# Probabilities transposed in 32x32 blocks by VectorE, value products over 32 rows, and a new order of the mixing stage

## The chip, the cores and the metric

The kernel runs on one core of a Trainium2 chip. It is one launch, and the metric is the device time in microseconds of that launch. The core's engines work side by side, each through its own queue in order: TensorE multiplies matrices into PSUM (eight banks of 128 x 512 float32), VectorE and ScalarE read PSUM and SBUF, GpSimd works on SBUF, and SyncE (SP) and GpSimd issue DMA transfers. They wait for each other by semaphores.

## The reference

One layer of an encoder with 512 tokens of width 1024: a half-weighted SwiGLU FFN, a mixing stage, a second such FFN, and a final RMSNorm. The mixing stage projects the normalized tokens once, gives 512 columns to a Fourier mixer and the rest to attention with eight query heads and two key/value heads of 64, and projects both back. Cut to the mixing stage and what attention computes:

```python
x = x + 0.5 * swiglu(rms_norm(x, ffn1_norm), ffn1_w_gate, ffn1_w_up, ffn1_w_down)
u = rms_norm(x, mix_norm) @ w_in
f_out = fourier_mixer(u[..., :512], fnet_w, fnet_b)
a_out = gqa_attention(u[..., 512:1024], u[..., 1024:1152], u[..., 1152:], q_norm, k_norm)
x = x + concatenate([f_out, a_out]) @ w_out
x = x + 0.5 * swiglu(rms_norm(x, ffn2_norm), ffn2_w_gate, ffn2_w_up, ffn2_w_down)
...
# gqa_attention, for a block of 128 queries (q and k normalized per head and rotated):
scores = einsum('bqhgd,bkhd->bhgqk', q_blk, k) * 64 ** -0.5
p = softmax(scores, axis=-1)
out = einsum('bhgqk,bkhd->bqhgd', p, v)
```

## The kernel before

All products are made with float32r operands that are split into a high part and a low rest (`.h` and `.l` operations; the helper `lows`, line 123, is the subtraction), so that a product is three matmuls: high x high, high x low, low x high (`product`, lines 164 to 166). The two FFNs hold x transposed, 128 features by 512 tokens in a tile; their larger groups use a seven-product scheme of 256 columns (line 429). They are the first 335 and the last 339 us of the program.

The mixing stage is written as some 640 small named operations, and the string `ORDER` names all of them in the order in which they are emitted; on each engine, DMA queues too, the instructions stand in that order. An operation's name tells what it does: `k.0` to `k.7`, `q0.0` and so on are the eight steps of a projection (three matmuls each), `q0.pq` sums of squares for a head's norm (four matmuls of two columns, in two passes each), `f00.0` and `f00.1` the halves of a Fourier projection (12 matmuls of 256 columns each, lines 1063 to 1065), `d..`, `map.` and `c..` the transform over positions and channels, `y0.0` to `y7.7` the steps of the output projection; `wq0.r`, `.h`, `.l` load a weight chunk and split it.

Attention goes by pairs: `t` (0 to 3) numbers query heads within a key/value head, `b` (0 or 1) is the key/value head, and `c` is one of four blocks of 128 queries. So there are 32 score tiles of 128 queries by 512 keys.

- `s{t}{b}{c}`: two matmuls of 512 columns (lines 1188, 1189) give a score tile in a PSUM bank.
- `m`: VectorE takes the negated maximum of the tile (line 1194) and multiplies it by the row's factor in `sc` (line 1195).
- `e`: ScalarE makes the exponentials (line 1202) into SBUF and sums them into `z`.
- `t{t}{b}{kc}`: TensorE transposes, for one block of 128 keys, the four query blocks of a head (four transposes of 128 x 128, line 1214) into a bank.
- `h`, `l`: ScalarE casts the bank into the high part `ph` (line 1219), VectorE subtracts for the rest `pl` (line 123).
- `v{t}{b}{kc}`: two matmuls of 512 columns (line 1257) with the stationary tile `vst`, which holds the values of one key block, high in columns 0 to 63 and low in 64 to 127; four key blocks accumulate in one bank.
- `o.c`, `o.a`, `z.r`, `z.w`, `z.p`, `r.m`, `r.h`, `r.l`: add the two halves, divide by the sums (GpSimd spreads them in `z.w`, TensorE transposes them), and split the result for the output projection.

The values are projected transposed, scaled by a row `n1.rb` that `n1.t` and `n1.b` make with four transposes and a copy, and transposed (`vt`, `vp`). GpSimd has little to do in the stage: powers (`.s1`, line 949), four copies, three transfers. PSUM banks come from one pool of eight and are handed out by `bank_for` and given back by `read`.

Of the kernel before, what the change touches and what calls it, by code (L numbers as in the profile page):

```python
# [37 lines left out]
HI_DVE = ("f0", "f1")  # L38
# [5 lines left out]
wk.r wq0.r wv.r cos wk.h wk.l wq0.h k.0 k.1 k.2 k.3 k.4 wv.h k.5 wq0.l k.6 wq1.r k.7 k.sq q0.0 wq1.h n1.c  # L44
k.rc n1.m k.sw n1.p q0.1 q0.2 q0.3 q0.4 wq1.l q0.5 wq2.r n1.t q0.6 q0.7 wq2.h q1.0 k.rs k.pq wv.l q0.sw
n1.b v.0 v.1 k.s0 k.s1 wq2.l q0.rc f2.r wq3.r q0.rs q0.ah q0.bh k.s2 v.2 kw v.3 v.4 v.5 v.6 q0.sq q0.al
q0.bl v.7 vt kp wq3.h km q1.1 wq3.l q0.pq f0.r q0.s0 k1.0 k0.0 k0.1 q1.2 q1.3 q1.4 q1.5 k1.2 k0.2 vp q1.6
q1.7 k0.3 s003 s001 s000 k1.1 k1.3 s010 f1.r v0.h v0.l q0.s1 q0.s2 f0.h m001 m003 s002 q1.sw m002 m010 q1.sq
q1.sd q1.pq e002 m000 v1.h e000 e001 e003 q2.0 q2.1 q2.2 q1.s0 q1.s1 f0.l q1.rc q1.rs v1.l q2.3 q2.4 q1.bh
q2.5 q2.6 q2.7 q2.sw t001 e010 f1.h f1.l q2.rc t000 q3.0 s012 h000 l000 s011 m011 t002 h002 h001 m012 q1.ah  # L50
q1.al q2.sq q3.1 q3.2 q3.3 q3.4 q3.5 q3.6 q1.bl q3.7 s013 l002 e011 v000 e012 f2.h l001 v001 q2.sd q3.sw
q2.rs t003 m013 q2.ah q3.rc q3.sq v002 e013 q2.bh f2.l s100 q1.s2 m100 s102 h003 q3.sd e100 f00.0 t010 f3.r
q2.bl h010 q2.pq l003 q2.s0 q2.s1 t013 m102 e102 s101 m101 f00.1 f00.u q2.al v003 l010 e101 t011 h011 q3.rs
s103 t012 f02.0 h013 l011 z0.r o00.c o00.a q3.bh v010 v011 m103 h012 l012 q3.pq q3.s0 l013 e103 s110 m110
s201 q3.ah s111 q3.bl v012 v013 o01.c t100 m111 h100 l100 e111 o0.r t101 h101 t102 h102 o01.a fw.r f02.1
e110 s112 m112 e112 z0.w pos q2.s2 l102 f01.0 s113 l101 z0.p m113 e113 s203 r0.m f02.e s200 m200 v100 v101
t103 t110 f01.1 r0.h h103 l103 z1.r f02.h v102 f01.u e200 q3.al q3.s1 v103 o10.c t112 m201 h110 r0.l h112
s202 m202 l110 t113 m203 f03.0 f03.1 v110 f3.h q3.s2 o10.a e201 s210 f03.e f3.l t111 l112 f10.0 f02.l h113
h111 l111 e202 f10.1 f03.h e203 s211 v111 m210 o2.r fw.h e210 t200 h200 t202 l113 m211 v112 s300 l200 v113
h202 t201 f10.u h201 l202 o11.c s212 m212 e212 s213 z1.w e211 f12.0 fw.l l201 f12.1 m300 e300 m213 e213  # L60
o11.a z1.p r1.m s301 v200 t203 r1.h f03.l h203 f12.e l203 f12.h z2.r z2.w v201 v202 t211 s302 m302 t210 h210
l210 s303 m303 h211 l211 v203 o20.c o20.a t212 h212 m301 f11.0 f13.0 e302 s311 l212 f12.l o0.h o0.l r1.l
t213 f11.1 f11.u m311 v210 v211 f13.1 h213 l213 f13.e e303 v212 s310 d00 m310 e301 t302 o1.r o1.h o1.l t301
f13.h f13.l e310 v213 o21.c t300 o21.a h302 l302 map0 map0.h map0.l d10 h300 l300 map1 z2.p d00.h map1.h
d00.l e311 t303 r2.m map1.l h303 l303 v300 s312 h301 m312 d20 d01 o2.h s313 d11 l301 v301 v302 v303 m313
e312 d01.h d01.l c0.s o2.l e313 t312 d11.h d11.l o30.c d31 o30.a h312 l312 o4.r c0.c c0.q c0.o t311 d10.h
t310 h311 h310 l310 d10.l d20.h d21 d20.l l311 c0.h c0.l d30 t313 c1.c d21.h d21.l o3.r c1.s c1.q d30.h v310
c1.o d31.h d31.l v311 v312 y1.0 h313 l313 c2.s z3.r z3.w c1.h o6.r d30.l c2.q c2.c y0.0 c2.o c2.h y2.0 c3.s
c3.q v313 r2.h c1.l z3.p c2.l c3.c c3.o y1.1 y2.1 y2.2 y0.1 r2.l y0.2 c3.h c3.l y2.3 y0.3 y1.2 y0.4 y0.5
y0.6 o31.c o31.a r3.m r3.h y1.3 y1.4 r3.l y0.7 o3.h y1.5 y2.4 y0.x y2.5 y2.6 o3.l y1.6 o5.r y1.7 o4.h y0.q  # L70
o4.l y1.x y1.q y2.7 o5.h o5.l y3.0 y1.a y3.1 y3.2 y3.3 y3.4 y3.5 y3.6 y3.7 y1.h o6.h o6.l y3.x y3.q y4.0
y4.1 y4.2 y2.x y2.q y4.3 y5.0 y4.4 y4.5 y4.6 y3.h y3.l o7.r y5.1 y5.2 y5.3 y4.7 y4.x y4.h y2.a y3.a o7.h
y6.0 o7.l y0.h y5.4 y5.5 y4.l y5.6 y4.q y4.a y5.7 y6.1 y6.2 y0.l y6.3 y6.4 y5.x y7.0 y6.5 y2.h y6.6 y6.7
y6.x y1.l y2.l y7.1 y6.q y7.2 y7.3 y7.4 y7.5 y7.6 y5.q y7.7 y6.h y6.l y5.h y5.l y5.a y7.x y7.q y6.a y7.h
y7.a y7.l
# [8 lines left out]
def encoder(ctx, tc, A, out):  # L84
# [15 lines left out]
    pp = ctx.enter_context(tc.tile_pool(name="psum", bufs=8, space=bass.MemoryType.PSUM))  # L100

    def bank(name):
        return pp.tile([P, S], F32, tag="bank", name=name)
# [18 lines left out]
    def lows(lo, src, hi):  # L122
        nc.vector.tensor_tensor(out=lo, in0=src, in1=asf(hi), op=ALU.subtract)  # L123
# [44 lines left out]
    class Norm:  # L168


        def __init__(self, n):
            self.n = n
            self.acc = tp.tile([P, S], F32, tag="acc", name=f"acc{n}")
            self.r = cp.tile([P, 4], F32, name=f"r{n}")
            self.ms = cp.tile([P, 4], F32, name=f"ms{n}")
            self.rb = cp.tile([P, S], F32, tag="rb", bufs=2, name=f"rb{n}")
# [628 lines left out]
    with tc.tile_pool(name="mix", bufs=1) as mp, tc.tile_pool(name="mixt", bufs=1) as mt:  # L805
# [36 lines left out]
        def read(name):  # L842
            held[name][1] -= 1
            if not held[name][1]:
                spare.append(held.pop(name)[0])
# [765 lines left out]
```

## Time and profile before

| | |
|---|---|
| time, median of 3 runs | 837.93 us (837.79 to 838.09) |
| the profiled execution's own time | 837.96 us |
| its span, first to last instruction | 836.2 us |
| mean granted TensorE clock | 0.999 |
| HBM read / written | 111.83 MB / 2.10 MB |
| mixing stage, within the span | 335.6 to 497.4 us |

The page gives busy time by engine; PE is TensorE's matmuls, PEld its weight loads, DVE VectorE, ACT ScalarE, POOL GpSimd. A group of instructions has its line, engine, operation, out<-in, shapes and count, then busy us and mean ns of one, then idle time before it and what ended that. On TensorE and VectorE, instructions overlap their successors, so the distance from start to start is shorter than the duration. The chain of waits goes back from the last instruction to what released each; a row there has a start, the time on the chain, and the line.

### The profile page before, as it was taken

Reading aid. Unit: us, or ns where it says so; the run is one execution under the profiler, and the core shown is the slowest. Engines: PE = TensorE matmul, PEld = TensorE weight load, DVE = VectorE, ACT = ScalarE, POOL = GpSimd, SP = SyncE. Lnnn points to the kernel's source line nnn. Section 1 sums busy time; section 2 is a strip of 40 time slices with the busy share of each in tenths; the row PEclk is TensorE's granted clock in tenths of the full one; section 3 lists DMA queues with packets and bytes.
Section 4 is the critical chain, followed back from the end, with each engine's and each line's share of the span. In section 5 each row is a group of like instructions: output and inputs, shape, how many; then the busy total and the mean of one; then the engine's idle time right before and its main releaser. Section 6 shows DMA issues by size and latency. Waiting matters only on the chain.

```text
span 836.2 us, 13649 instructions
## 1 busy us (share of the span) xinstructions
PE 829.4 (99%) x5418; PEld 752.3 (90%) x5418; DVE 603.4 (72%) x923; ACT 461.9 (55%) x770; POOL 62.5 (7%) x69
## 2 busy tenths in 40 slices
PE   9999999999999999999999999999999999999997
PEld 7888998899989998889999888899988999899986
DVE  7977884578656867699999478878755885578563
ACT  7654763366434644677776446546533663356452
POOL 0111000000000000222000000110000000000001
PEclk9999999999999999999999999999999999999999
DMA  7787765468365423414020326777554674456122
GB/s 253 189 199 191 199 187 147 117 159 226 97 169 151 121 58 114 151 51 146 26 76 26 100 57 170 187 182 197 165 154 125 179 206 131 116 167 189 45 78 101
DMA packets 46110, 117.16 MB, mean 140 GB/s; under 512 B 5216, under 2 KB 9952, under 8 KB 45920
## 3 DMA queue, kind: packets, MB, share of 16 engines
q1 hardware_dynamic: 38128, 92.57, 33.5%
q0 software_dynamic: 7648, 23.47, 16.4%
q8 instruction: 42, 0.69, 0.3%
q10 hardware_dynamic: 272, 0.26, 0.1%
q14 instruction: 20, 0.16, 0.1%
HBM read 111.83 MB, written 2.10 MB: 136 GB/s over the span
## 4 chain that ended last, share of the span: by engine, by line
PE 99%; issue 0%; DVE 0%; POOLq 0%; POOL 0%; ACT 0%
PE r L429 23%; PE q L429 11%; PE dn L166 9%; PE dn L164 9%; PE dn L165 9%; PE p L429 6%; PE mix L164 4%; PE mix L166 3%; PE mix L165 3%; PE gu L766 3%; PE gu L164 3%; PE gu L165 3%; PE gu L166 3%; PE mix L1257 2%; PE mix L1214 2%; PE mix L1188 1%
## 5 line engine op out<-in xcount | busy, mean ns | idle before, releaser
L429 PE MATMUL r<-rt,ring 128*128 128x256 f32 x1686 | 204.9, 276 | 0.0
L429 PEld LDWEIGHTS r<-rt,ring 128*128 128x128 f32 x1686 | 198.5, 188 | 0.9
L165 PE MATMUL dn<-at,ring 128*128 128x512 f32 x295 | 114.8, 389 | 0.0
L166 PE MATMUL dn<-at,ring 128*128 128x512 f32 x295 | 114.8, 389 | 0.0
L164 PE MATMUL dn<-at,ring 128*128 128x512 f32 x295 | 114.8, 389 | 0.0
L429 PE MATMUL q<-rt,ring 128*128 128x256 f32 x840 | 106.6, 276 | 0.0
L374 ACT CAST ring<-s 128x1024 fp32r<-128x1024 f32 x70 | 73.5, 1050 | 58.3 <-DVE s L394 51.5
L581 DVE SCALAR_TENSOR_TENSOR gx<-dn,gx 128x512 f32<-128x512 f32 x61 | 42.1, 691 | 81.1 <-PE dn L166 81.1
L429 PEld LDWEIGHTS q<-rt,ring 128*128 128x128 f32 x840 | 100.4, 188 | 0.0
L123 DVE TENSOR_TENSOR ring<-s,ring 128x1024 fp32r<-128x1024 f32 x70 | 85.3, 1219 | 0.6 <-ACT ring L374 0.6
L156 ACT CAST ring<-raw_dn 128x768 fp32r<-128x768 f32 (+2 forms) x48 | 40.7, 852 | 75.6 <-PE dn L165 70.5
L166 PEld LDWEIGHTS dn<-at,ring 128*128 128x128 f32 x295 | 55.4, 188 | 11.5
L165 PEld LDWEIGHTS dn<-at,ring 128*128 128x128 f32 x295 | 55.4, 188 | 11.1
L164 PEld LDWEIGHTS dn<-at,ring 128*128 128x128 f32 x295 | 55.4, 188 | 11.0
L346 POOL DMA_DIRECT2D s<-in_wgu x35 | 30.1, 861 | 423.5 <-DVE ring L123 146.7
L429 PE MATMUL p<-rt,ring 128*128 128x256 f32 x420 | 53.3, 276 | 0.0
L123 DVE TENSOR_TENSOR ring<-raw_dn,ring 128x768 fp32r<-128x768 f32 (+2 forms) x48 | 46.7, 977 | 7.1 <-ACT ring L156 7.1
L429 PEld LDWEIGHTS p<-rt,ring 128*128 128x128 f32 x420 | 50.2, 188 | 0.0
L123 DVE TENSOR_TENSOR ring<-raw_g,ring 128x1024 fp32r<-128x1024 f32 x35 | 42.6, 1217 | 0.0
L123 DVE TENSOR_TENSOR at<-u,at 128x512 fp32r<-128x512 f32 x35 | 24.2, 693 | 20.3 <-ACT at L484 20.2
L472 DVE TENSOR_TENSOR u<-g,u 128x512 f32<-128x512 f32 x35 | 24.0, 687 | 19.8 <-ACT u L469 19.8
L374 ACT CAST ring<-raw_g 128x1024 fp32r<-128x1024 f32 x35 | 36.8, 1051 | 0.0
(312 smaller groups left out, 1523.0 us busy)
## 6 DMA issues: line engine op xcount, KB each, us to landing
s<-in_wgu SPq DMA_DIRECT2D x70, 256.0 KB, 4.2
s<-in_wgu POOLq DMA_DIRECT2D x35, 512.0 KB, 5.7
raw_g<-in_wgu SPq DMA_DIRECT2D x35, 512.0 KB, 4.0
raw_dn<-in_wd SPq DMA_DIRECT2D x44, 384.0 KB, 3.9
raw_u<-in_wgu SPq DMA_DIRECT2D x35, 256.0 KB, 4.1
raw_gu<-in_wgu SPq DMA_DIRECT2D x12, 512.0 KB, 3.5
raw_o<-in_wo SPq DMA_DIRECT2D x8, 512.0 KB, 3.6
raw_dn<-in_wd SPq DMA_DIRECT2D x5, 448.0 KB, 4.2
```

The source lines that it names most:

```text
L123: nc.vector.tensor_tensor(out=lo, in0=src, in1=asf(hi), op=ALU.subtract)
L156: nc.scalar.copy(hi[:, :n, :], raw[:, :n, :])
L164: nc.tensor.matmul(ps, whi, mhi, start=first, stop=False)
L165: nc.tensor.matmul(ps, whi, mlo, start=False, stop=False)
L166: nc.tensor.matmul(ps, wlo, mhi, start=False, stop=last)
L346: nc.gpsimd.dma_start(out=blocks(t), in_=up, accum_op=ALU.add)
L374: nc.scalar.copy(ts[0], src)
L429: nc.tensor.matmul(ps[:, c], a[:, ks], b[:, i, c], start=first and i == 0 and o == 0, stop=i == KH - 1 and o == 2, skip_group_check=not fi ...
L472: nc.vector.tensor_tensor(out=self["u"], in0=self["g"], in1=self["u"], op=ALU.mult)
L581: nc.vector.scalar_tensor_tensor(out=x[d][:, t], in0=ps[:, t], scalar=0.5, in1=x[d][:, t], op0=ALU.mult, op1=ALU.add)
L766: nc.tensor.matmul(pss[c], w[:, k % 2, c], m[k], start=k == 0 and m is hh and w is hi, stop=k == KD - 1 and w is lo,)
L1214: nc.tensor.transpose(pts[n][:, c * P : (c + 1) * P], prob[t, b, c][:, kc * P : (kc + 1) * P], ident)
```

## The change

What it does, all in the mixing stage but for the banks:

- Transposes of probabilities leave TensorE. `x{t}{b}{c}` is one VectorE instruction that transposes each 32x32 block of an exponentials tile, from SBUF to SBUF. `h` and `l` now read that tile, and write into `its`, which holds the eight tiles of a set: key/value head `b`, two query heads, four query blocks.
- `p{st}`, one for each of four sets, takes the place of 64 value products: 128 matmuls, each over 32 rows (32 keys), with a stationary tile of 32 x 128 and 256 moving columns (8 tiles x 32 queries), on rows 0 to 31, 32 to 63, 64 to 95 and 96 to 127 in turn. Row group `a` has queries 32a to 32a+31 of each block, and accumulates in its own bank `quad[:, a]`. The instruction's tile is 32 x 128, and its position in the array the row group's.
- The stationary values must lie in each of the four row groups: `vr{v}.{a}` copies `stage[v]` into `vrep` with four transfers on GpSimd's queue, 16 for each value head. `vrep` and `its` exist once.
- `m` is one instruction: it multiplies the score tile by the (negated) factor, in its bank, and keeps the minimum. `e` then has the constant scale -1.
- Values are scaled after their transpose (`vm`, by column `n1.r`); `n1.t` and `n1.b` are gone.
- `LOWS_POOL` gives 23 of the 32 probability differences, eight weight differences of 1024 columns and one of 512 to GpSimd; `z.w` goes to ScalarE; `HI_DVE` names other casts for VectorE.
- The eight banks are fixed tiles, four of them one tile `quad`; all stages rotate over them.
- cos, sin, and buffers of the early part share room with the tables of the late part, and `ORDER` is another.

```diff
-HI_DVE = ("f0", "f1")
+LOWS_POOL = """
+001 010 012 013 100 103 110 111 112 113 200 201 202 203 211 212 300 301 302 303 310 311 312 f1 f2 fw o0 o1 o2 wq2
+wq3 wv
+""".split()
+SUMS_ACT = """
+z0 z1 z2 z3
+""".split()
+HI_DVE = """
+300 302 o3 o5 wq2 wv
+""".split()
...
-    pp = ctx.enter_context(tc.tile_pool(name="psum", bufs=8, space=bass.MemoryType.PSUM))
+    pp = ctx.enter_context(tc.tile_pool(name="psum", bufs=1, space=bass.MemoryType.PSUM))
+    quad = pp.tile([P, 4, S], F32, name="quad")
+    quads = [quad[:, i] for i in range(4)]
+    singles = [pp.tile([P, S], F32, name=f"bank{i}") for i in range(4)]
+    turn = singles[1:] + quads + singles[:1]
...
+            def spread(a):
+                for i in range(4):
+                    src, dst = slice(32 * i, 32 * i + 32), slice(32 * a, 32 * a + 32)
+                    nc.gpsimd.dma_start(
+                        out=vrep[dst].rearrange("p (c i) e -> p c i e", i=4)[:, :, i],
+                        in_=stage[v][src].rearrange("p c o e -> p c (o e)"),
+                    )
...
-                nc.vector.tensor_reduce(out=mx, in_=sps[n], axis=AX.X, op=ALU.max, negate=True)
-                nc.vector.tensor_tensor(out=mx, in0=mx, in1=f, op=ALU.mult)
+                nc.vector.tensor_scalar(
+                    out=sps[n], in0=sps[n], scalar1=f, scalar2=None, op0=ALU.mult, op1=ALU.min, accum_out=mx
+                )
...
-                for c in range(4):
-                    nc.tensor.transpose(pts[n][:, c * P : (c + 1) * P], prob[t, b, c][:, kc * P : (kc + 1) * P], ident)
...
+                nc.vector.transpose(turned[n], probs[n])
+
+            op(f"h{n}")(lambda: (nc.vector.tensor_copy if n in HI_DVE else nc.scalar.copy)(ph, turned[n]))
+            op(f"l{n}")(lambda: lows(pl, turned[n], ph, nc.gpsimd if n in LOWS_POOL else nc.vector))
...
+            @op(f"p{st}")
+            def _():
+                all_quads(f"p{st}", 4)
+                for j in range(16):
+                    for o in range(2):
+                        for a in range(4):
+                            rows = slice(32 * a, 32 * a + 32)
+                            nc.tensor.matmul(
+                                quad[:, a, : 8 * 32], vrep[rows, j], its[rows, o, :, 32 * j : 32 * j + 32],
+                                start=j == 0 and o == 0, stop=j == 15 and o == 1, skip_group_check=True,
+                            )
...
-                w = vst[:, b, kc].rearrange("p a e -> p (a e)")
-                for i, p in enumerate(parts[n]):
-                    nc.tensor.matmul(outs[t, b], w, p, start=kc == 0 and i == 0, stop=kc == 3 and i == 1)
```

How the new order moves instructions shows best in three places. The first is TensorE's queue in the middle of attention. Before (`mix` are PSUM banks, `ks` the keys, `qa` and `qb` the queries, `ph` and `pl` the transposed probabilities' parts, `e` the exponentials):

```order
L1188 MATMUL mix_3411<-ks_3420,qb_3714 128x512
L1189 MATMUL mix_3411<-ks_3421,qb_3714 128x512
L1257 MATMUL mix_3416<-ph_3964,vst 128x512
L1257 MATMUL mix_3416<-pl_3966,vst 128x512
L1257 MATMUL mix_3416<-ph_3947,vst 128x512
L1257 MATMUL mix_3416<-pl_3975,vst 128x512
L1214 MATMUL mix_3409<-ident,e_3853 128x128
L1214 MATMUL mix_3409<-ident,e_3919 128x128
L1214 MATMUL mix_3409<-ident,e_3893 128x128
```

And in the change, at the second set of value products (`bank` and `quad` are banks; line 1239 is the score product, 1278 the value products, 1319 the transpose of the sums):

```order
L1239 MATMUL bank_72<-ks_3315,qb_3329 128x512
L1240 MATMUL bank_72<-ks_3316,qb_3329 128x512
L1278 MATMUL quad<-its,vrep 128x256 x128
L1239 MATMUL bank_70<-ks_3315,qb_3329 128x512
L1240 MATMUL bank_70<-ks_3316,qb_3329 128x512
L1319 MATMUL bank_71<-ident,zw_4127 128x128 x4
L1239 MATMUL bank_73<-ks_3315,qb_3331 128x512
```

Value products stood in pairs, one pair for each transposed tile; now 128 of them stand together, and the first can start only when all eight tiles of the set are split.

The second place is VectorE's queue in the same part, before:

```order
L1194 TENSOR_REDUCE mx_3981<-mix_3413 128x1
L1195 TENSOR_TENSOR mx_3981<-mx_3981,sc 128x1
L123 TENSOR_TENSOR qb_3955<-rot_q_3827,qb_3955 64x512
L1194 TENSOR_REDUCE mx_4000<-mix_3411 128x1
L1195 TENSOR_TENSOR mx_4000<-mx_4000,sc 128x1
L123 TENSOR_TENSOR pl_4005<-mix_3409,ph_4003 128x512
```

and in the change, ahead of the third set (`x` is the block-wise transposed tile, `fo` a channel sum of the Fourier mixer, `el` its rest, `ring` the buffer of its positions):

```order
L1245 TENSOR_SCALAR bank_72,mx_4614<-bank_72,sc 128x512
L1263 STREAM_TRANSPOSE x_4616<-e_4584 128x512
L1245 TENSOR_SCALAR bank_71,mx_4620<-bank_71,sc 128x512
L1263 STREAM_TRANSPOSE x_4758<-e_4596 128x512
L1245 TENSOR_SCALAR bank_73,mx_4760<-bank_73,sc 128x512
L1307 RECIPROCAL zall<-zall 128x8
L1263 STREAM_TRANSPOSE x_4782<-e_4618 128x512
L136 TENSOR_TENSOR el_3326<-fo_4607,eh_3322 128x512
```

A maximum with its small product and a difference per tile became a minimum and a transpose per tile; most differences are gone from this queue.

The third place is GpSimd's queue, where they went. In the change, between the first and the third set (`more` and `raw_o` belong to an output weight):

```order
L136 TENSOR_TENSOR its<-x_4199,its 128x512
L136 TENSOR_TENSOR its<-x_4224,its 128x512
L136 TENSOR_TENSOR more<-raw_o_3922,more 128x1024
L1071 DMA vrep<-vst 32x4x128 x4
L136 TENSOR_TENSOR its<-x_4384,its 128x512
L1071 DMA vrep<-vst 32x4x128 x4
L136 TENSOR_TENSOR its<-x_4406,its 128x512
```

Before, GpSimd's queue between the tables' transfers and the second FFN held one power and three copies of sums. Now differences stand among the transfers that replicate the second value head, and the transfers wait until the second set's products have read the first.

More of the change, by code (lines that the diff above doesn't have):

```diff
@@ L54 @@
[L54 to L58, printed above, removed]
@@ L833, in op @@
             return put
[L836 removed]
+        spare, held = [(b, any(b is q for q in quads)) for b in turn], {}
         def bank_for(name, readers=1):
[L839 to L840 removed]
+            i = next((i for i, b in enumerate(spare) if not b[1]), 0)
+            held[name] = [spare.pop(i), readers]
+            return held[name][0][0]
         def read(name):
```

284 lines of the change are left out of this document (147 added, 137 removed).

## The prediction

> **What bounds the kernel now.** I read the page's busy times and chain first, then a table of three stretches of the mixing stage, then TensorE's waits.
>
> ```profile
> PE 829.4 (99%) x5418; PEld 752.3 (90%) x5418; DVE 603.4 (72%) x923; ACT 461.9 (55%) x770; POOL 62.5 (7%) x69
> ...
> PE 99%; issue 0%; DVE 0%; POOLq 0%; POOL 0%; ACT 0%
> ```
> ```profile
> 335.60:381.40 45.80, 45.80 (x233) 38.45 (x232) 38.08 (x70) 33.00 (x56) 9.12 (x4) 1.00 0.28 94
> 381.40:455.10 73.70, 73.70 (x527) 67.70 (x527) 69.36 (x148) 56.73 (x119) 7.82 (x9) 1.00 0.24 77
> 455.10:497.40 42.30, 42.30 (x192) 35.13 (x191) 24.41 (x34) 17.02 (x26) 0.00 (x0) 1.00 0.25 75
> ```
> ```profile
> PE busy L705 <- DVE halves L735: 1.0, 1, 1.0
> ```
>
> The columns of the second fence are the stretch, its length, and busy time of TensorE, its weight loads, VectorE, ScalarE and GpSimd. The mixing stage runs from 335.6 to 497.4, 161.8 us, and TensorE is busy in all of it; its only wait for another engine in the whole program is 1.0 us at the start. So a microsecond of TensorE work that goes is a microsecond gained, as long as the others keep up. Stretch A (the projections) and C (the output projection) have slack: VectorE is busy 38.08 of 45.80 and 24.41 of 42.30. Stretch B, from the first Fourier projection to the last value product, has little: VectorE is busy 69.36 of 73.70, 94%. B cannot become much shorter unless VectorE gets rid of work there. I cost the FFN stages and the fixed banks at nothing: TensorE's instructions there are the same in the same order over the same eight banks, and it waits for nobody. VectorE and ScalarE swap a few operations in the first FFN; if a reused bank came late for that, a matmul would wait for one more eviction, 0.6 us (VectorE's step, below), a few times at most.
>
> **TensorE's prices.** From the chain of waits (start, time on the chain, line) and the groups:
>
> ```profile
> 379.55 0.44 PE mix L1214 x4
> 379.99 0.47 PE mix L1257 x2
> 380.46 0.24 PE mix L1188
> ...
> 383.21 0.79 PE mix L935 x8
> ...
> 405.99 0.11 PE mix L1064
> ```
> ```profile
> L1214 PE MATMUL mix<-ident,e 128*128 128x128 f32 x128 | 18.1, 273 | 0.0
> L1257 PE MATMUL mix<-ph,vst 128*128 128x512 f32 x32 | 13.0, 406 | 0.0
> L1257 PE MATMUL mix<-pl,vst 128*128 128x512 f32 x32 | 12.6, 392 | 0.0
> ...
> L429 PE MATMUL q<-rt,ring 128*128 128x256 f32 x840 | 106.6, 276 | 0.0
> ```
>
> A transpose takes 0.109 us of the chain (0.44 for four), a matmul of 512 columns 0.23, one of 256 columns 0.113 (the rows alternate between 0.11 and 0.12). The group's mean ns are longer, because matmuls overlap; the chain has the time that each takes from the next. Removed: 128 transposes of probabilities, 14.0 us; 64 value products, 14.7; four transposes of n1's row, 0.44. Added: 512 matmuls over 32 rows and 256 columns. Nothing in this trace has 32 rows; every group says 128*128. Bounds from the nearest row, the 256-column matmul: if four of them, on disjoint quarters of the array and in four banks, run side by side, 512 x 0.113 / 4 = 14.5 us; if they run one behind the other, 512 x 0.113 = 57.9 us. I take 14.5: it equals the 14.7 of the value products that they replace, which is the same number of multiplications on a full array, and row groups, banks and replicated values are separate for all four. The other end is a rival. The switch between 32 and 128 rows, eight times, is not in the trace either; bounds are nothing and the overlap that would be lost once, 0.276 - 0.113 = 0.16 us, so up to 1.3 us, of which only the pair in C, 0.3 us, lies where TensorE sets the end.
>
> [...]
>
> With these prices TensorE's work in A is 48 projection steps of three matmuls (33.1), five small sums of 0.79 (4.0), two transposed tiles (0.9) and eight score tiles of two matmuls (3.7): 41.6 us. In B: 192 Fourier matmuls (21.7), 24 score tiles (11.0), positions, maps and channels (10.5), one small sum, three transposed tiles (2.1), 13 output steps (9.0), three of the four sets of value products (10.9): 65.2. In C: the fourth set (3.6), 51 output steps (35.2), 0.4: 39.3. The sum is 146.1, where the same count for the kernel before gives 160.9 against 161.8 in the trace.
>
> **VectorE.** Its instructions overlap too, so the price is the distance between starts:
>
> ```profile
> 440.56 0.68 DVE L123 TENSOR_TENSOR pl<-mix,ph 128x512 fp32r<-128x512 f32 x1
> 441.16 0.68 DVE L1194 TENSOR_REDUCE mx<-mix 128x1 f32<-128x512 f32 x1
> 441.87 0.16 DVE L1195 TENSOR_TENSOR mx<-mx,sc 128x1 f32<-128x1 f32 x1
> 441.95 0.68 DVE L123 TENSOR_TENSOR pl<-mix,ph 128x512 fp32r<-128x512 f32 x1
> ...
> 443.75 1.22 DVE L123 TENSOR_TENSOR ring<-raw_o,ring 128x1024 fp32r<-128x1024 f32 x1
> 444.88 0.42 DVE L123 TENSOR_TENSOR ring<-mix,ring 128x255 fp32r<-128x255 f32 x1
> ```
> ```profile
> L1194 DVE TENSOR_REDUCE mx<-mix 128x1 f32<-128x512 f32 x32 | 21.8, 682 | 1.2 <-PE mix L1189 1.1
> ...
> L987 DVE COPY kw<-sc 128x512 f32<-128x512 f32 x1 | 0.4, 427 | 0.0
> ```
>
> A difference (hi/lo split) of 512 columns costs 0.60, of 1024 columns 1.13, a maximum with its small product 0.79. The new ones are not in the trace. A 32x32 block transpose of 512 columns lies between a copy (0.43) and a maximum with its exposed end (0.71); I take 0.60, as the differences have. The scaled minimum, one instruction over the same bank in place of two, lies between 0.60 and 0.79; I take 0.70. In B, by the order of the change, that makes 28 transposes more (+16.8), 20 probability differences fewer because GpSimd has them (-12.0), three weight differences of 1024 and one of 512 fewer (-4.0), 24 minima for 23 maxima (-1.4), and +3.0 for pieces that moved between stretches (three more channel splits, one more channel sum, two casts, less small ones): +2.4, so 69.4 becomes 71.8. **VectorE has more to do in B than TensorE, 71.8 against 65.2.** B now lasts at least 71.8; if VectorE idles for the same 4.3 us as now, 76.1. I take the middle, 74.0. What is late then is each set of value products: it waits for the splits of all eight tiles of a set, and scores and output steps stand behind it in TensorE's queue. ScalarE (56.73 of 73.70) keeps its count of operations, and SP its transfers.
>
> **GpSimd** takes the differences over, and issues the copies that replicate the values. Its rows:
>
> ```profile
> 367.45 2.54 POOL L949 TENSOR_TENSOR sc<-sc,mhalf 128x8 f32<-128x8 f32 x1 [6.33 <-DVE sc L945]
> 384.88 1.64 POOL L949 TENSOR_TENSOR sc<-sc,mhalf 128x8 f32<-128x8 f32 x1 [14.88 <-DVE sc L945]
> ...
> 390.02 0.61 POOL L1239 COPY zw<-z 128x512 f32<-128x512 f32 x1 [3.51 <-ACT qb L973]
> ...
> 391.19 0.55 POOL L1369 DMA_DIRECT2D pos<-in_pos  x1
> ...
> 403.07 1.03 POOL L1239 COPY zw<-z 128x512 f32<-128x512 f32 x1 [9.04 <-DVE z L1234]
> ```
> ```profile
> L1390 POOL TENSOR_TENSOR gx<-gx,rb 128x256 f32<-128x256 f32 x2 | 1.5, 744 | 2.4 <-ACT rb L246 2.4
> ```
> ```profile
> s<-in_wgu SPq DMA_DIRECT2D x70, 256.0 KB, 4.2
> ```
>
> The copies are 32 issues of some 0.55 us (the pos row), 18 us of GpSimd's time. The first sixteen are early. The other sixteen overwrite the first value head's copies, so they wait for the second set's products, and the third set waits for them: 16 x 0.55 = 8.8 us and a landing of about 4, beside 13 us of TensorE's work from one set to the next, so they hide, barely.
>
> A two-input operation of 256 columns took 0.744, so 512 columns lie between that and 1.49; I take 1.34, and 2.5 for 1024. In B that is 22 probability tiles, the half-size weight and four weights, 41 us of 74: it fits, but the rows show something else. The same power takes 1.64 or 2.54, the same copy 0.61 or 1.03: GpSimd is held by something while VectorE is busy. If VectorE is held in turn, some 26 of its operations in B read two SBUF tiles; each would meet a busy GpSimd 41 times in 74 and wait half of its 1.34: 9.6 us. The other bound is nothing. VectorE's maxima do not spread (682 mean) because GpSimd is idle now. I take a third, 3.2. B becomes 77.2.
>
> The sum: A 45.8 to 41.6 (-4.2), B 73.7 to 77.2 (+3.5), C 42.3 to 39.3 (-3.0), a switch in C (+0.3): -3.4. From the profiled execution's 837.96 us (span 836.2; the median of the runs is 837.93) that gives **834.6**: 15 us less work for TensorE, of which VectorE and GpSimd take back three quarters.
>
> **Rivals.**
> *GpSimd and VectorE hold each other* in B, and the kernel is slower. With the full 9.6 us and all the idle time, B lasts 85.7, +12.0: 837.96 - 4.2 + 12.0 - 3.0 + 0.3 = 843.1. It decides from B at 80.6. For it speak the spread of GpSimd's rows and the 94%; against it, that only 26 of VectorE's operations read SBUF twice. [...]
>
> *The 32-row matmuls do not run side by side.* Each has a weight load of its own (5418 loads for 5418 matmuls), and the matmul of two columns shows the least that such a pair takes: 0.79 / 8 = 0.099. With that price the sets cost 512 x 0.099 = 50.4, 35.9 more than assumed: B 65.2 + 26.9 = 92.1, C 48.3, A 41.6, 182.0 in place of 161.8: 858. With 0.113 each, 866. Against it stands only the layout of the operands.
>
> *VectorE runs ahead*: block transposes nearer 0.43, no lock, and work done in A's slack. Then TensorE's sum holds, 146.1 scaled by 161.8 / 160.9 to 146.9: 823.1. For it: 7.7 us of VectorE's idle time in A. Against: that slack is early, before scores exist.
>
> **How the numbers follow.** The forecast 0.50, held by each other 0.22, not side by side 0.13, running ahead 0.15. A measurement tells 0.2%, 1.7 us, from no change. The forecast's own range, from B at 71.8 plus nothing to B near 84, is 829 to 841: 0.40 faster, 0.08 same, 0.02 slower. The first rival gives 0.04 same and 0.18 slower, the second 0.13 slower, the third 0.15 faster. Faster 0.55, same 0.12, slower 0.33. The range for 8 in 10 leaves out the second rival and a little at both ends: 824 to 846.
>
> **What would show it.** Starts of the new matmuls 0.03 us apart, 3.6 us a set, against 0.1 apart. TensorE with idle time in B, before the sets of value products, ended by VectorE or GpSimd, 8 to 15 us of it; VectorE busy for all of B; none in A and C. Block transposes near 0.60 from start to start; GpSimd's differences near 1.34, and VectorE's two-SBUF differences longer than 0.68 where GpSimd is at work. I am wrong if TensorE has no idle time, if the sets take over 5 us each, or if the FFN stages move by over 1 us.

## The result, and the profile after

The changed kernel takes **969.73 us** (967.42 to 971.27, four runs) against 837.86 (837.72 to 838.09): ratio 1.157, 95% interval 1.1545 to 1.1598. The forecast was 834.6, with 846 as the upper end.

The page after, busy time by engine and the chain's share by engine:

```profile
PE 872.2 (90%) x5734; PEld 765.8 (79%) x5734; DVE 614.6 (63%) x927; ACT 457.9 (47%) x770; POOL 127.1 (13%) x129
...
PE 77%; DVE 12%; ACT 4%; issue 3%; DMA 3%; SPq 0%; POOL 0%; DVEq 0%; POOLq 0%; ACTq 0%
```

TensorE was 99% of the chain before. Now 23% of it is other engines or waiting for them. Where that lies shows in a table of the three stages (length; busy time of TensorE, weight loads, VectorE, ScalarE, GpSimd, each with its number of instructions; granted clock, DMA share, GB/s). Before:

```profile
0.00:335.60 335.60, 334.61 (x2188) 303.29 (x2189) 239.36 (x344) 181.00 (x291) 22.29 (x29) 1.00 0.58 160
335.60:497.40 161.80, 161.80 (x948) 141.27 (x947) 131.85 (x250) 106.74 (x200) 16.94 (x13) 1.00 0.25 81
497.40:836.20 338.80, 332.99 (x2285) 307.73 (x2283) 232.20 (x329) 174.18 (x281) 23.26 (x27) 1.00 0.55 148
```

After:

```profile
0.00:386.15 386.15, 352.17 (x2189) 308.29 (x2189) 240.09 (x344) 180.97 (x291) 22.17 (x29) 1.00 0.51 139
386.15:574.20 188.05, 166.81 (x1263) 141.90 (x1262) 139.31 (x252) 101.28 (x197) 81.55 (x73) 0.92 0.29 80
574.20:969.50 395.30, 353.24 (x2285) 315.60 (x2283) 235.24 (x332) 175.69 (x283) 23.35 (x27) 0.98 0.47 127
```

The two FFN stages, which the change does not touch but for their banks, have the same numbers of matmuls (2188 and 2189 in the records of the first, 2285 in both of the second) and take 50.5 and 56.5 us more. The mixing stage, where all the other work was done, takes 26.3 more. TensorE's longest waits in the whole program (us in total, times, longest) and the two groups of the seven-product matmuls, by the tile that they write:

```profile
PE quad L177 <- DVE gx L598: 14.7, 17, 0.9
PE quad L446 <- ACT p L454: 14.0, 28, 1.0
PE quad L446 <- DVE g L493: 8.7, 14, 1.2
PE quad L446 <- DVE g L478: 5.7, 10, 0.6
```
```profile
L446 PE MATMUL quad<-rt,ring 128*128 128x256 f32 x1516 | 202.6, 283 | 36.2 <-ACT p L454 14.0
...
L446 PE MATMUL bank<-rt,ring 128*128 128x256 f32 x1430 | 174.8, 278 | 0.0
```

Of these products, only those that go to `quad`, the one tile of four banks, wait; 1430 of the same matmuls into the four single banks wait for nothing. The timeline shows one such wait after another (start, duration, instructions, idle time and what ended it):

```profile
87.49 1.74 PE L446 MATMUL quad<-rt,ring 128*128 128x256 f32 x13 [0.88 <-DVE gx L598]
89.27 0.37 ACT L454 COPY p<-quad 128x256 f32<-128x256 f32 x1 [2.01 <-PE quad L446]
89.69 1.65 PE L446 MATMUL quad<-rt,ring 128*128 128x256 f32 x12 [0.46 <-ACT p L454]
91.37 0.37 ACT L454 COPY p<-quad 128x256 f32<-128x256 f32 x1 [1.74 <-PE quad L446]
91.80 1.65 PE L446 MATMUL quad<-rt,ring 128*128 128x256 f32 x12 [0.46 <-ACT p L454]
```

These are p1, p5 and p2 of the seven products. p1 goes to one bank, p5 to another, p2 to a third. p5 and p2 each start only when ScalarE has copied the result before it out of *its* bank. A product of twelve matmuls comes every 2.11 us in place of 1.36 (12 x 0.113): 0.46 is idle time, and the product itself takes 1.65, because its first matmul starts 0.22 before the second and the end of its last no longer overlaps the next product.

What the prediction spoke of in the mixing stage is there. A set of 32-row products, in the changed kernel:

```profile
461.65 4.12 PE L1278 MATMUL quad<-its,vrep 32*128 32x256 f32 x128 [0.74 <-ACT e L1254]
465.70 0.50 PE L1239 MATMUL bank<-ks,qa 128*128 128x512 f32 x1
```

128 matmuls in 4.05 us, 0.032 from one to the next, where a matmul of 256 columns over 128 rows takes 0.113: the four row groups run side by side. The second set, at 486.56, took 5.52, with the granted clock at half for most of it (0.50 from 487 to 489, mean 0.70).

### The profile page after: what moved, and what is told of

Read it like the earlier page. It is cut to its first block, busy times and chain, and to the rows that moved or that the text cites. A ratio compares the mean times of both kernels' runs of the same rounds, so it can differ in the third digit from the quotient of the medians.

```text
span 969.5 us, 14441 instructions
## 1 busy us (share of the span) xinstructions
PE 872.2 (90%) x5734; PEld 765.8 (79%) x5734; DVE 614.6 (63%) x927; ACT 457.9 (47%) x770; POOL 127.1 (13%) x129
## 4 chain that ended last, share of the span: by engine, by line
PE 77%; DVE 12%; ACT 4%; issue 3%; DMA 3%; SPq 0%; POOL 0%; DVEq 0%; POOLq 0%; ACTq 0%
PE quad L446 19%; PE bank L446 15%; PE bank L177 7%; PE bank L178 7%; PE bank L179 7%; PE quad L177 5%; PE quad L179 5%; PE quad L178 5%; DVE ring L136 2%; DVE gx L598 2%; PE quad L1278 2%; ACT p L454 1%; DMA s<-in_wgu 1%; PE bank L1471 1%; DVE s L411 1%
## 5 line engine op out<-in xcount | busy, mean ns | idle before, releaser
L446 PE MATMUL quad<-rt,ring 128*128 128x256 f32 x1516 | 202.6, 283 | 36.2 <-ACT p L454 14.0
L446 PEld LDWEIGHTS quad<-rt,ring 128*128 128x128 f32 x1516 | 184.3, 188 | 50.4 <-ACT p L454 19.6
L446 PE MATMUL bank<-rt,ring 128*128 128x256 f32 x1430 | 174.8, 278 | 0.0
L446 PEld LDWEIGHTS bank<-rt,ring 128*128 128x128 f32 x1430 | 169.5, 188 | 0.2
L177 PE MATMUL quad<-at,ring 128*128 128x512 f32 x157 | 63.0, 402 | 20.1 <-DVE gx L598 14.7
L598 DVE SCALAR_TENSOR_TENSOR gx<-quad,gx 128x512 f32<-128x512 f32 x32 | 22.1, 692 | 69.8 <-PE quad L179 69.8
L178 PE MATMUL quad<-at,ring 128*128 128x512 f32 x157 | 61.2, 390 | 0.0
L179 PE MATMUL quad<-at,ring 128*128 128x512 f32 x157 | 61.1, 389 | 0.0
L177 PEld LDWEIGHTS quad<-at,ring 128*128 128x128 f32 x157 | 29.4, 187 | 33.8 <-ACT ring L169 12.7
L179 PE MATMUL bank<-at,ring 128*128 128x512 f32 x138 | 53.8, 390 | 0.0
L178 PE MATMUL bank<-at,ring 128*128 128x512 f32 x138 | 53.8, 390 | 0.0
L177 PE MATMUL bank<-at,ring 128*128 128x512 f32 x138 | 53.7, 389 | 0.0
L598 DVE SCALAR_TENSOR_TENSOR gx<-bank,gx 128x512 f32<-128x512 f32 x29 | 20.0, 692 | 38.7 <-PE bank L179 38.7
L489 DVE TENSOR_TENSOR u<-g,u 128x512 f32<-128x512 f32 x35 | 24.0, 687 | 26.3 <-ACT u L486 26.3
```

The costliest lines, as they stand in the source:

```text
L177: nc.tensor.matmul(ps, whi, mhi, start=first, stop=False)
L178: nc.tensor.matmul(ps, whi, mlo, start=False, stop=False)
L179: nc.tensor.matmul(ps, wlo, mhi, start=False, stop=last)
L446: nc.tensor.matmul(ps[:, c], a[:, ks], b[:, i, c], start=first and i == 0 and o == 0, stop=i == KH - 1 and o == 2, skip_group_check=not fi ...
L489: nc.vector.tensor_tensor(out=self["u"], in0=self["g"], in1=self["u"], op=ALU.mult)
L598: nc.vector.scalar_tensor_tensor(out=x[d][:, t], in0=ps[:, t], scalar=0.5, in1=x[d][:, t], op0=ALU.mult, op1=ALU.add)
```

## The experiments

**Is it the four-bank tile?** Three kernels ask this, and `eight`, below. The first is the kernel before with only the banks of the change, handed out in the change's turn:

```diff
-    pp = ctx.enter_context(tc.tile_pool(name="psum", bufs=8, ...))
+    pp = ctx.enter_context(tc.tile_pool(name="psum", bufs=1, ...))
+    quad = pp.tile([P, 4, S], F32, name="quad")
+    quads = [quad[:, i] for i in range(4)]
+    singles = [pp.tile([P, S], F32, name=f"bank{i}") for i in range(4)]
+    turn = singles[1:] + quads + singles[:1]
```

> The kernel before with nothing of the change but its banks: one tile of four banks and four tiles of one, handed out in the change's turn. Theory one, a matmul into one bank of the four-bank tile waits until another bank of that tile has been read: both FFN stages grow as they did in the change, 335.6 to about 386 and 339 to about 395, and the mixing stage grows a little too; 940 to 965 us. Theory two, the FFN stages are slow because of the new order of the mixing stage, the operations that moved between VectorE and ScalarE, or a lower clock: nothing of that is here, so 838, within 3.

1006.2 us, ratio 1.200 (1.198 to 1.203). Its FFN waits are those of the changed kernel, and its mixing stage adds others:

```profile
PE quad L435 <- ACT p L443: 14.0, 28, 1.0
PE quad L170 <- DVE gx L587: 12.8, 15, 0.9
PE quad L435 <- DVE g L482: 9.9, 15, 1.2
...
PE quad L1194 <- ACT e L1208: 4.2, 2, 2.8
```

It is 41 us over the upper end of what the first theory said, and slower than the whole change, because its mixing stage meets the tile too (384.1 to 623.4, 239 us in place of 162). The FFN stages take 384.1 and 379.8. Nothing else of the change is needed for the loss in the FFN stages.

The second gives the FFN stages eight tiles of one bank, from pools of their own, and leaves the mixing stage its `quad`:

> The changed kernel with eight tiles of one bank in both FFN stages; the mixing stage keeps its four-bank tile. Theory one (whole tile): the FFN stages go back to 335.6 and 339, the mixing stage stays at 188; 865, within 5. Rival, banks come round too early in the fixed turn, whatever the tiles: the turn is the same length, so 955 to 970.

870.52 us (ratio 1.035 to 1.040), 0.5 over the first theory's range: 99.2 us of the 131.9 go. It has two waits of its own at the borders of the stages (0.9 and 3.5 us), where pools change hands.

The third keeps the tile and changes the turn only:

```diff
-    turn = singles[1:] + quads + singles[:1]
+    turn = [t for p in zip(singles[1:] + singles[:1], quads) for t in p]
```

> The changed kernel, only the turn is another: single bank, quarter of the four-bank tile, single, quarter, and so on. Theory one: successive products less often land in the four-bank tile together, so the FFN stages lose about half of their 106 us of growth: 900 to 935. Rival (a bank is taken again too early after eight hands): the distance between two uses of a bank is the same eight, so 955 to 970.

950.53 us. Better than the change by 19, so the turn matters, but 15 over the first theory's upper end. The group says why:

```profile
L446 PE MATMUL quad<-rt,ring 128*128 128x256 f32 x1450 | 192.6, 282 | 28.4 <-DVE g L478 8.7 <-ACT p L454 7.0 <-DVE g L493 6.0
```

The waits for p fell by half (14.0 to 7.0), those for VectorE's sums did not (`g`, 8.7 and 6.0 in place of 8.7 and 5.7). r, q and p2 are taken one after the other, so with the alternation r and p2 lie in the same tile, and u2, which goes to r, waits for the sum that reads p2. My half was counted without that.

**Eight tiles everywhere.** The results of a set are then read bank by bank:

```diff
-    quad = pp.tile([P, 4, S], F32, name="quad")
-    quads = [quad[:, i] for i in range(4)]
+    quads = [pp.tile([P, S], F32, name=f"quad{i}") for i in range(4)]
...
-                o, _, l = halves_of(t)
-                nc.scalar.copy(o, l)
+                for a in range(4):
+                    o, _, l = halves_of(t, a)
+                    nc.scalar.copy(o, l)
```

> The changed kernel with eight tiles of one bank everywhere; the two halves of each set's result are read bank by bank, by 64 small instructions in place of 16. Theory one: as with eight tiles in the FFN stages alone, and in the mixing stage the waits for other banks of the four-bank tile go too, some 4 to 6 us, with what the lower clock after them costs; the small instructions give back 3 to 6 us on VectorE: 845 to 866. Rival (turn): 955 to 970.

851.17 us (ratio 1.013 to 1.018), 118.6 us under the change, and the same work for the other engines. Its stages:

```profile
0.00:336.37 336.37, 335.38 (x2189) 303.78 (x2189) 239.30 (x344) 180.95 (x291) 22.28 (x29) 1.00 0.59 160
336.37:504.48 168.11, 156.26 (x1264) 133.28 (x1263) 139.98 (x276) 102.77 (x221) 81.78 (x73) 0.98 0.33 90
504.48:849.00 344.52, 336.25 (x2285) 310.11 (x2283) 234.18 (x332) 175.64 (x283) 23.32 (x27) 0.99 0.55 146
```

The first FFN stage is within 0.8 us of before. The mixing stage is 6.3 over its 161.8 and the second FFN stage 5.7 over its 338.8. The next runs look for these.

**The second FFN stage.** Where `eight` enters it, the sum of squares over the row (TensorE, 2 columns) waits for VectorE's last `acc`. In the order, y5's square `y5.q` came early and its sum `y5.a` last of all, and squares have two buffers. The change that mends it, in `ORDER`:

```diff
- ... y4.4 y5.q y4.5 y1.l ... y4.a y7.4 y7.5 y7.6 y7.7 y6.q y7.x y7.h y6.a y7.l y7.q y7.a y5.a
+ ... y4.4 y5.q y4.5 y5.a y1.l ... y4.a y7.4 y7.5 y6.q y7.6 y6.a y7.7 y7.x y7.q y7.h y7.a y7.l
```

A first try moved `y5.a` only to just before y7.6, and the last two sums ahead of the last splits:

> Eight tiles of one bank, and in the order's last row y5.a stands before y7.6 in place of last, and the last two squares and sums before the last splits. With eight tiles the second FFN stage still takes 344.5 against 338.8 before. Theory one, that is the sum of squares: y5's square holds one of two buffers until its sum, which stood last, so the squares of y6 and y7 and the row's sum come late: it goes back to 339 to 340, and the kernel to 845 to 847. Rival, the stage starts late because its first weights are split late by VectorE and ScalarE: no change, 850 to 852.

847.04 us (ratio 1.009 to 1.013). In the profiled execution, the slowest of the four (849.96), the stage still took 344.0 (504.21 to 848.2), against 344.5 in `eight`. Where the other three, 846.2 to 847.1, gained is not shown. The timeline:

```profile
508.75 0.39 PE L178 MATMUL quad<-ring 128*128 128x512 f32 x1
510.93 1.71 PE L235 MATMUL quad<-ones,acc 128*128 128x2 f32 x8 [1.80 <-DVE acc L1359]
512.50 0.77 PE L176 MATMUL quad<-ring 128*128 128x512 f32 x1
513.07 0.63 PE L177 MATMUL quad<-ring 128*128 128x512 f32 x1
513.50 0.63 PE L178 MATMUL quad<-ring 128*128 128x512 f32 x1
```

A wait of 1.8 us, and behind it matmuls that start 0.43 us apart in place of 0.23, at a granted clock of 0.50 (511.2 to 517.9). The diff above goes the whole way:

> As the kernel with eight tiles of one bank, but y5.a stands right behind y5.q, so y5's square gives its buffer back before the squares of y3 and y4 are made, and y6's square and sum stand before y7's last steps. With y5.a before y7.6 the row's sum still waited 1.8 us, and 12 matmuls behind it ran at 0.43 us a step in place of 0.23. Theory: the wait was the queue of squares behind two buffers, so it goes below 0.5 us and the slow matmuls with it, and the second FFN stage takes 339 to 341 against 344: 842 to 845. Rival: VectorE's splits of the first weights stand between, and it stays at 846 to 848.

845.62 us (845.31 to 845.83; ratio 1.007 to 1.010). The wait is 0.4 us, the granted clock 1.00 (509 to 518), and no matmul behind it is slow:

```profile
509.44 1.05 PE L235 MATMUL quad<-ones,acc 128*128 128x2 f32 x8 [0.36 <-DVE acc L1359]
510.36 0.48 PE L176 MATMUL quad<-ring 128*128 128x512 f32 x1
510.67 0.40 PE L177 MATMUL quad<-ring 128*128 128x512 f32 x1
```

The stage takes 339.3 (504.16 to 843.5). So the order of the squares and their sums was the cause; the kernel's time is just above the range that I gave it.

**The mixing stage: is VectorE held, or only busy?** In `eight`, TensorE's longest wait there is 4.0 us, for `sc`. What VectorE and GpSimd did before it:

```profile
371.24 6.58 POOL L1070 DMA_DIRECT2D vrep<-its  x12 [0.25 <-DVE its L135]
...
377.13 4.36 DVE L980 SCALAR_TENSOR_TENSOR sc<-sc,r 128x8 f32<-128x8 f32 x1
...
377.80 2.41 POOL L135 TENSOR_TENSOR ring<-raw_f,ring 128x1024 fp32r<-128x1024 f32 x1
380.19 1.27 POOL L135 TENSOR_TENSOR its<-x,its 128x512 fp32r<-128x512 f32 x1
...
385.10 0.42 PE L1109 MATMUL bank<-ring 128*128 128x256 f32 x1 [3.98 <-DVE sc L969]
```

A product of 128 x 8, 0.16 us in the kernel before, took 4.36: it ended with the second of two GpSimd instructions that stood one behind the other (380.19 + 1.27 = 381.46). It began 0.67 us before the first of them, while GpSimd issued the last transfers of `vrep`; what held it in that time is not shown. The next kernels test whether GpSimd's differences hold VectorE, as a lock would. All differences of the mixing stage back on VectorE (`LOWS_POOL` empty, `tail`'s order):

> As the kernel with the changed last row, but VectorE makes all differences of the mixing stage; GpSimd keeps powers, copies and issues. Theory one, lock: VectorE's rows that were stretched (sc 1.5, its 0.88, ring<-gx 1.0, rot_q 1.2 us) go back to 0.16, 0.68, 0.75 and 0.68, 13 us in all; but it gets 23 differences of 512 at 0.60 and nine weight differences of 1024 at 1.13 (one of 512), 23 us, 16 to 17 of it in the middle stretch: 4 to 12 us slower than the kernel with the changed last row. Rival, GpSimd's help costs as much as it gives: within 3 us. If VectorE's rows stay stretched, it was no lock.

858.14 us (ratio 1.023 to 1.027), 11.1 over `tail`, within the first theory's 4 to 12. VectorE's rows in `eight` (first two) and here:

```profile
L980 DVE SCALAR_TENSOR_TENSOR sc<-sc,r 128x8 f32<-128x8 f32 x5 | 7.6, 1512 | 1.8 <-POOL sc L976 1.8
L135 DVE TENSOR_TENSOR its<-x,its 128x512 fp32r<-128x512 f32 x9 | 7.7, 878 | 0.0
```
```profile
L978 DVE SCALAR_TENSOR_TENSOR sc<-sc,r 128x8 f32<-128x8 f32 x5 | 0.8, 161 | 1.9 <-POOL sc L974 1.9
L133 DVE TENSOR_TENSOR its<-x,its 128x512 fp32r<-128x512 f32 x32 | 21.0, 671 | 0.0
```

So GpSimd's differences held VectorE: without them the same operations are short again, though GpSimd still makes powers and issues transfers. I call this the lock. GpSimd's help is still worth more than it costs.

But the wait that led here is mostly not the lock's. In `no_pool` the row takes 0.16 (376.21), and TensorE still waits 3.7 us for `sc`:

```profile
378.91 0.69 DVE L948 TENSOR_TENSOR sw_q<-sw_q,early 128x512 f32<-128x512 f32 x1 [1.59 <-DMA sw_q<-early]
383.46 0.58 PE L1107 MATMUL bank<-ring 128*128 128x256 f32 x1 [3.72 <-DVE sc L967]
```

VectorE now waits for a transfer in the place where it was held before, and then makes what stands ahead of `sc` in its queue. TensorE goes on at 383.5 in place of 385.1.

Only the weights' differences back on VectorE:

> As the kernel with the changed last row, but GpSimd keeps only the 23 differences of probability tiles; VectorE makes the nine differences of weights. Theory one, the lock: GpSimd's longest instructions (2.4 us and more) are gone, so no VectorE row is held over 1.6 us, the wait for sc shrinks from 4.0 to 2 or less, but VectorE has 9 to 10 us more work in all, 4 of it in the middle stretch: within 3 us of the kernel with the changed last row. Rival, VectorE's work alone decides: 4 to 8 us slower.

848.31 us (ratio 1.011 to 1.014), 1.3 over `tail`, within what the lock's theory said. The wait for `sc` shrank to 3.0, not to 2, and VectorE still had a row of 2.2 us, so these two parts of the theory missed. Then s2 alone off VectorE:

```diff
-                nc.vector.scalar_tensor_tensor(out=v, in0=v, scalar=factor, in1=rx, op0=ALU.mult, op1=ALU.mult)
+                r = n1.r if factor == 1.0 else n1.rs   # n1.rs: n1.r times the factor, made once
+                nc.gpsimd.tensor_tensor(out=v, in0=v, in1=r.unsqueeze(2).to_broadcast([P, 4, 2]), op=ALU.mult)
```

> As the kernel with the changed last row, and the small product after each power (s2, 128 x 8, two SBUF operands) is made by GpSimd right behind its power, not by VectorE. Theory one, VectorE is held while GpSimd runs an instruction: these five rows of 1.5 us (one 4.4, until two differences of GpSimd had ended) go, and with them TensorE's wait of 4.0 us for sc and the slow matmuls behind it: 4 to 7 us under the kernel with the changed last row. Rival, VectorE is late there by its work, not by a lock: the wait moves to another of its results, within 1.5 us of that kernel.

842.55, 843.25, 852.42 and 852.60 us: a median of 847.8 (ratio 1.005 to 1.018), which tells nothing from `tail`. Two of the four agree with the first theory. The profile is of one near 852. In it the wait for `sc`, which that theory had as gone, is still 3.8 us, and another row is caught, a 512-column difference that takes 0.69 elsewhere, and here outlasts four GpSimd instructions, the last of which ended at 443.15 + 2.33 = 445.48:

```profile
439.42 6.62 DVE L135 TENSOR_TENSOR el<-fo,eh 128x512 fp32r<-128x512 f32 x1
439.44 3.75 POOL L135 TENSOR_TENSOR its<-x,its 128x512 fp32r<-128x512 f32 x3
443.15 2.33 POOL L135 TENSOR_TENSOR ring<-raw_o,ring 128x1024 fp32r<-128x1024 f32 x1
```

The same with `tail2`'s order, and with GpSimd's weight differences taken away too:

> The same with s2 made by GpSimd. Theory one, a VectorE row that meets GpSimd waits until GpSimd's whole train of instructions behind one another has ended, and which row that is varies between executions: two groups of times again, as 842.5 and 852.5 before, each 3 to 5 us lower: 838 to 840 and 847 to 850. Rival, the times vary for another reason (a clock, a transfer): one group.

> The same with s2 on GpSimd, and GpSimd keeps only the 23 differences of probability tiles. Its trains are shorter, so no VectorE row above 3 us and less spread between executions; VectorE has 9 us more work, 4 in the middle stretch: 841 to 846. Rival, VectorE's work alone decides there: 846 to 850.

The first: 842.1 and 843.6, and four between 847.3 and 848.3. Two groups, as the lock has it, but only the upper one is lower than in `s2_pool`; 838 to 840 did not come. The profile is again of the upper group, with the same row at 6.60 and a wait of 5.0 us on TensorE for it, behind which the granted clock was 0.50 for 6.8 us (445.0 to 451.8). The second, without GpSimd's long instructions, has no row of that kind and takes 843.86 (842.05 to 844.39; ratio 1.0048 to 1.0074), as its first theory said; it is still slower than before.

Does GpSimd let VectorE in at an instruction that reads nothing? Behind each difference of GpSimd, a memset of one column:

> As the kernel with s2 on GpSimd and the sums earlier; behind each difference GpSimd sets one column of a scratch tile to zero. Theory one, VectorE is let in at an instruction of GpSimd that reads nothing: no VectorE row is held longer than one difference (2.4 us at most), the held rows cost half, and the times are one group, 836 to 841. Rival, the lock is kept as long as GpSimd has an instruction ready, whatever it is: rows of 4 to 7 us stay, and the times are those of the kernel without the extra instructions or 1 to 3 us above.

870.21 us. In its profile the row stays, through four differences with a memset behind each; the first two:

```profile
450.10 6.77 DVE L136 TENSOR_TENSOR el<-fo,eh 128x512 fp32r<-128x512 f32 x1
450.18 1.30 POOL L136 TENSOR_TENSOR its<-x,its 128x512 fp32r<-128x512 f32 x1
451.43 0.09 POOL L138 MEMSET pause<- 128x1 f32 x1
451.48 1.26 POOL L136 TENSOR_TENSOR its<-x,its 128x512 fp32r<-128x512 f32 x1
```

But neither theory had 870: every stage was longer than in `s2_tail2`, the two FFNs by some 11 us each. The scratch column had moved all tiles behind it by 4 bytes. Writing into a filler tile instead, and the same 4 bytes in the kernel before, tell the pauses from the 4 bytes:

> The run with a pause after each difference of GpSimd, but the pause writes into a filler tile that is there anyway, so that no tile lies elsewhere. Theory one, the 4 bytes made the 870 us: 842 to 849, as without pauses, with the same held rows of up to 6.6 us. Rival, the pauses cost it: 865 to 872.

> The kernel before with one unused column of 4 bytes ahead of its tiles. Theory one, tiles 4 bytes further slow TensorE's matmuls by 2.2% (0.2317 from 0.2267 us a step of 512 columns in the run with the pauses): 855 to 860. Rival, the shift does nothing: 838.

843.29 (841.40 to 848.55; ratio 1.004 to 1.009) and 860.70 us (ratio 1.025 to 1.028). The pauses cost nothing and gain nothing that can be told: five of the seven times lie at 841.4 to 843.5 and two near 848, where `s2_tail2` had two of six low. The theory's held rows of 6.6 us are not in this profile, which is of the lowest time, 841.40. In it the same row began 0.36 us into a difference and was let in at its end, ahead of the next one, which took 1.71 in place of 1.29:

```profile
439.60 1.29 POOL L134 TENSOR_TENSOR its<-x,its 128x512 fp32r<-128x512 f32 x1
439.96 1.48 DVE L134 TENSOR_TENSOR el<-fo,eh 128x512 fp32r<-128x512 f32 x1
...
440.87 1.71 POOL L134 TENSOR_TENSOR its<-x,its 128x512 fp32r<-128x512 f32 x1
```

TensorE's longest wait for VectorE's splits is 1.6 us here, and 5.0 in `s2_tail2`. So both profiles of the upper group have the long row and this one of the lower group does not. The memset is not what lets the row in: in `eight`, without any, it began inside a difference too (443.00) and took 1.41.

The 4 bytes cost the kernel before 22.4 us. TensorE is busy 852.1 us in place of 829.4, which is the whole difference. The same group of matmuls in the kernel before, without and with them:

```profile
L165 PE MATMUL dn<-at,ring 128*128 128x512 f32 x295 | 114.8, 389 | 0.0
```
```profile
L165 PE MATMUL dn<-at,ring 128*128 128x512 f32 x295 | 116.5, 395 | 0.0
```

**Is VectorE's own work the rest?** Four weights' rests made by ScalarE and an adding transfer, in `s2_tiles_tail2`:

> As the kernel whose GpSimd keeps only the tile differences (843.9), but the rests of four weights of the middle stretch (f1, f2, o0, o1) are made by ScalarE (a negated copy of 1.05 us) and a transfer that adds, not by VectorE (1.13 us each). Theory one, VectorE's work is the bound of the middle stretch: 4.5 us less of it, 3 to 4.5 us of time: 839 to 841. Rival, the lock and the order decide where TensorE waits, or ScalarE takes VectorE's place: 843 to 847.

845.49 us (five runs, 840.88 to 848.47; ratio 1.006 to 1.011): no gain over the 843.86 without. The theory's 3 to 4.5 us did not come, so VectorE's work alone is not what holds the last 6 us, or the transfers' issues on GpSimd give it back; that stays open. The same with seven weights (`dma7`; the theory said 836 to 839) took 849.30 us (848.13 to 850.77) and had a TensorE wait of 5.2 us for a weight's transfer. Its results are not the layer's, so it decides nothing. No version here beats the kernel before.

## Why the prediction was wrong, point by point

- **The step that failed** stands in the first part: "I cost the FFN stages and the fixed banks at nothing: TensorE's instructions there are the same in the same order over the same eight banks, and it waits for nobody." The instructions, order and banks were as said. What I priced was a bank that is *reused* late, "0.6 us, a few times at most". What happened is a wait for the reader of a *neighbour*: the program's waits are made for tiles, and four banks were now one tile. With eight tiles, 118.6 of the 131.9 us are gone, 99.2 of them by the FFN stages alone. I read the line `quad = pp.tile([P, 4, S])` as a layout. This one step makes nine tenths of the loss; without it the kernel would still have missed the forecast, by 16.6 us (851.17 against 834.6), for the reasons below.
- **The 32-row products: right.** 4.05 us a set at full clock against 3.6; four sets 16.2 against 14.5, where one behind the other would be 57.9. The extra 1.7 is the term's error. The measured ratio is 57.9 / 16.2 = 3.6, and the rival that they do not run side by side is out.
- **VectorE's new rows: right.** In `eight` the block transposes stand 0.63 apart (0.60 forecast), the scaled minima 0.67 (0.70). GpSimd's differences took 1.35 and mostly 2.4 (1.34 and 2.5).
- **VectorE bounds the middle stretch: right in kind.** In `eight` it is busy 92% or more of each 10 us from 380 to 450, 77.2 us in B against the forecast's 75.0 (71.8 and 3.2), and TensorE waits there.
- **The lock: mechanism right, too small and in the wrong place.** I took a third of 9.6 us, 3.2, all in B. From the mean rows of `eight` less those of `no_pool` it is 14.0 us of VectorE's time: 6.8 in five small products that I had not counted among the operations with two SBUF operands, 2.1 in `ring<-gx`, 1.9 in `its`, 3.2 in others. Row by row, about 5.5 of it lie in B, between my 3.2 and the 9.6 of the bound, and 8.5 in A, where I had priced none. Of the nine rows that were held longest, seven ended with the one difference of GpSimd that they met, and only the 4.36 outlasted two. Rows that read a bank or a single SBUF tile kept their length: 25 minima took 740 ns in `eight` and 741 in `no_pool`, the block transposes 694 and 696. I had put the maxima's steady 682 down to an idle GpSimd; beside a busy one, the minima's mean did not move. The first rival's number, 843.1, is nearer to the kernel with eight tiles (851.2, or 845.6 with the order mended) than my forecast, but this is partly luck: it put 85.7 on B, which took 79.6, and nothing on A.
- **Stretches.** In `eight` B, from the first Fourier projection to the fourth set, takes 79.6 (77.2 forecast), and C 39.8 (39.6). B holds two stretches of 3.4 us in which the granted clock was half, one right behind the wait for `sc`. A takes 48.7 in place of 41.6: 5.9 us of it are TensorE's waits for VectorE, 4.0 of them at its very end for `sc`. The held row explains only part of these, as `no_pool` still waits 3.7 there. I had forecast no wait in A. This is the second step that failed: of the 16.2 us between the forecast and the profiled execution of `eight` (850.82), 7.1 lie in A, 2.4 in B, 0.2 in C, 0.8 in the first FFN stage and 5.7 in the second.
- **Not foreseen: the order's end.** y5.a at the end of the order cost the second FFN stage 5.2 us (344.5 in `eight`, 339.3 in `tail2`). I counted the sums that moved and not which buffer they hold.
- My own test of failure, FFN stages that move by over 1 us, was the right one to name. I gave it no chance of its own.

## What to carry to other kernels

When buffers are merged into one tile, list who reads each part and what is next written into another part: each such pair is a new wait, also in stages that the change does not touch. Price a meeting of two engines wherever both work, not only in the stretch that one of them bounds: 8.5 of the 14 us lay where VectorE had slack. Before putting a wait down to a lock, look whether it goes when the lock goes: the one for `sc` went from 4.0 to 3.7. And before believing a small regression, look whether a tile's address moved.

## What the runs showed of the hardware that was not expected

- **Four bytes.** With the tiles behind one spare column 4 bytes further, and nothing else changed, the matmuls of 512 columns in the kernel before went from 389 to 395 ns, at a granted clock of 0.998, and the kernel from 838.3 to 860.7, 2.7%. No run here varied the shift, so the cause is not shown.
- **Held through several instructions, at times.** A VectorE row that takes 0.69 us elsewhere lasted 6.77, through four differences of GpSimd with memsets between them. Most held rows ended with one difference (1.41 us in `eight`, 1.48 in `spaced_in_room`, for the same operation). The rows of 4.36, 6.62 and 6.77 began 0.67, 0.02 and 0.08 us before GpSimd's first difference, behind transfers that it issued; whether that decides it is not shown.
- **The clock behind a wait of 1.8 us.** In `tail`, TensorE was idle for 1.80 us, and the granted clock was 0.50 from 511.2, 0.3 us after the eight 2-column matmuls behind the wait began (mean 0.89 from 500 to 530). These took 1.71 us in place of 1.05, and the 12 matmuls after them started 0.43 us apart in place of 0.23, so those alone cost another 2.4. In `tail2`, after 0.36 us, the clock stayed at 1.00 and none was slow. In `no_pool` the same wait was 1.80 us too, but the eight matmuls behind it took 1.05, the next ones started 0.23 apart, and the clock was 1.00 from 500 to 530. So the length of the wait alone does not tell whether the clock falls, and what does is not shown.
